# Fillers in the layer norms, eight-tile groups that end bank by bank, and the estimated mean taken off tile by tile

## The chip, the cores and the metric

The kernel runs on one core of a Trainium2 chip. The metric is the device time of one execution in microseconds (us). A core has engines that run side by side: TensorE (PE in the profile, PEld for its weight loads), VectorE (DVE), ScalarE (ACT), GpSimd (POOL) and SyncE (SP), whose queue issues the weight transfers here. Each engine works through its instructions in order and waits on semaphores for the others. PE's clock is granted by a throttle; the profile shows it as PEclk, as a share of full speed.

## The reference, cut to what matters

The kernel computes a decoder trunk of two layers on one sequence of 256 tokens with 2048 features, in float32. Each layer has a mixer and a feed-forward block, and after each of them the sum with the residual is normalised (post-norm):

```python
x = LN(alpha * x + gate * mixer(mod(x)))        # o0, o1: the mixer's output projection
x = LN(alpha * x + gate * swiglu(mod(x)))       # g.., d..: gate/up and down projections
mu  = mean(x); var = mean((x - mu) ** 2)
LN  = (x - mu) * rsqrt(var + 1e-5) * g + b
```

`mod` scales and shifts by vectors that come from the conditioning vector c (adaLN), and `gate` is one of them too. Layer 0's mixer is a forgetting attention beside a state-space layer, layer 1's a sliding-window attention with rotary positions. So there are four norms: after o0, after the feed-forward of layer 0 (ending with d01), after o1 and after d11. The first three feed a projection, the last one the output.

## The kernel before, in words

Everything is kept transposed: features lie in the 128 partitions, tokens in 256 columns, so the 2048 features are 16 tiles of 128 x 256 (`z`). The weights are streamed from HBM once, in pieces of 128 x 1024 float32 (512 KB) on SP's queue into a ring of nine buffers. Each piece is split into a rounded part `wh` (ACT, L269) and the rest `wl` (DVE, L270), and the activations lie in two parts `hi` and `lo` as well (`hp`). A product of a weight tile with an activation tile is then three passes of 256 columns: `wh*hi`, `wh*lo`, `wl*hi` (`mm3`, L609 to L611), or, where the output has a bank to itself, one pass of 512 columns and one of 256 (`mm2`, L614 and L615). In c1 and c2 the activations are the stationary side (L1346). A piece makes a **unit** of eight weight tiles; splits run two units ahead (`LOOK`), with three split buffers.

`_plan` lists the phases and their groups of output tiles: ..., o0, g00, d00, g01, d01, c1, c2, o1, g10, d10, g11, d11. Four PSUM banks of 512 columns accumulate (`acc`), and four (`aux`) serve everything else. Inside a group the tiles go k-outer (one k, all outputs, then the next k) or o-outer (one output to its end, then the next). An output tile is evacuated one unit after its last product (`c.later(1, ...)`): for o0, o1 and d.. tile by tile (`evac_slot`, then `z_evac`, which adds bank x gate to `z`, L950), for g.. as a whole group (`evac_group`, Silu on ACT and the product on DVE, L1279).

A **norm** runs while its sub-layer's outputs come in. After the first four tiles their mean is estimated (`ln_shift`: a product with ones, L986, a copy to SBUF, L988) and subtracted from all sixteen tiles in one burst of 16 subtractions (L992), since a shift by any constant leaves the norm as it is and keeps the sums of squares small. Then each tile is squared (ACT, L970) and added to the sums S1 and S2 (DVE, L976 to L980; `ln_stat`). After the last tile `ln_tail` brings the sums over the partitions with products of one column (L1008, `total`), forms the mean (L1031), the variance (L1033, L1034) and 1/sigma (ACT L1035; DVE L1037 to L1039), and spreads mean and 1/sigma over the partitions (L1013, `spread`). `ln_tile` then normalises tile by tile (L1055, L1064, L1067, L1068, L1075) into the next projection's `hp`. While it does so, nothing else is there for PE: the next projection waits for the first `hp`.

The order of instructions on each engine is set by a scheduler, which simulates a timeline and picks among what is ready; `c.front` gives an instruction a token (pe, act, front, load) by which those of one token keep their written order and go ahead of others. In the norm before c1, DVE also prepares the rotary positions (`rope_prep`, L1088 and on), whose input is loaded there by a transfer from ACT's queue (L1083).

## Time and profile before

| | |
|---|---|
| Time, three runs | 2271.1 us median (2271.01 to 2273.81) |
| The profiled execution | 2271.06 us; its span 2269.3 us, so 1.8 us lie around the span |
| Mean granted clock of PE | 0.988 |
| Busy: PE, DVE, ACT | 2214.3, 1705.1 and 1137.0 us (98%, 75%, 50%) |
| HBM read | 576.43 MB, 255 GB/s over the span |

A row of a group or of the timeline reads: start, duration, engine, line, operation, output <- inputs by the program's names, shape, the count of instructions joined in the row, and in brackets how long the engine stood idle before it and what released it. A row of a window reads: from:to, length, then for PE, PEld, DVE, ACT and POOL the busy time and the count, then PEclk, the share of the DMA engines that were busy and GB/s. Durations of PE overlap: products that take 0.28 us each start 0.12 us apart, so paces are read from start to start.

### The profile page before, as it was taken

Reading aid. Unit: us, or ns where it says so; the run is one execution under the profiler, and the core shown is the slowest. Engines: PE = TensorE matmul, PEld = TensorE weight load, DVE = VectorE, ACT = ScalarE, POOL = GpSimd, SP = SyncE. Lnnn points to the kernel's source line nnn. Section 1 sums busy time; section 2 is a strip of 40 time slices with the busy share of each in tenths; the row PEclk is TensorE's granted clock in tenths of the full one; section 3 lists DMA queues with packets and bytes.
Section 4 is the critical chain, followed back from the end, with each engine's and each line's share of the span. In section 5 each row is a group of like instructions: output and inputs, shape, how many; then the busy total and the mean of one; then the engine's idle time right before and its main releaser. Section 6 shows DMA issues by size and latency. Waiting matters only on the chain.

```text
span 2269.3 us, 37524 instructions
## 1 busy us (share of the span) xinstructions
PE 2214.3 (98%) x14362; PEld 1912.8 (84%) x14362; DVE 1705.1 (75%) x3026; ACT 1137.0 (50%) x1838; POOL 2.3 (0%) x6
## 2 busy tenths in 40 slices
PE   6999999999999999999999999999999999999997
PEld 4878887789888888888888878799888888888886
DVE  7649877888888888888886988787776555555576
ACT  3456565366444434444444766575444334444444
POOL 0000000000000000000000000000000000000000
PEclk8999999999999999999999999999999999999998
DMA  9988787858998889998874776358877556656662
GB/s 335 365 334 320 277 303 269 325 170 296 316 321 318 320 317 318 319 320 320 315 252 161 272 273 207 120 159 269 269 266 245 186 186 186 190 190 185 188 186 73
DMA packets 161476, 580.99 MB, mean 256 GB/s; under 512 B 18448, under 2 KB 18960, under 8 KB 160912
## 3 DMA queue, kind: packets, MB, share of 16 engines
q1 hardware_dynamic: 159984, 575.49, 73.7%
q10 hardware_dynamic: 1312, 3.11, 0.4%
q8 instruction: 112, 1.84, 0.3%
q14 instruction: 68, 0.56, 0.1%
HBM read 576.43 MB, written 2.10 MB: 255 GB/s over the span
## 4 chain that ended last, share of the span: by engine, by line
PE 93%; DVE 3%; ACT 2%; DMA 1%; issue 1%; ACTq 0%; SPq 0%; DVEq 0%
PE acc L614 43%; PE acc L615 22%; PE acc L1346 6%; PE acc L609 5%; PE acc L610 4%; PE acc L611 4%; PE ab L656 1%; PE aux L562 1%; DVE wl L270 1%; DVE w L540 1%; PE aux L1202 1%; PE aux L1169 0%; ACT wh L269 0%; DMA w<-in_ada 0%; PE tr L512 0%
## 5 line engine op out<-in xcount | busy, mean ns | idle before, releaser
L614 PE MATMUL acc<-hp,wh 128*128 128x512 f32 x4212 | 1465.3, 397 | 3.6 <-DVE z L950 2.4
L270 DVE TENSOR_TENSOR wl<-w,wh 128x1024 fp32r<-128x1024 f32 (+1 forms) x712 | 862.5, 1212 | 411.7 <-ACT wh L269 395.8
L269 ACT CAST wh<-w 128x1024 fp32r<-128x1024 f32 (+1 forms) x712 | 740.4, 1041 | 830.8 <-PE acc L614 462.5
L615 PE MATMUL acc<-hp,wl 128*128 128x256 f32 x4212 | 1149.3, 280 | 0.5 <-DVE wl L270 0.5
L614 PEld LDWEIGHTS acc<-hp,wh 128*128 128x128 f32 x4212 | 778.6, 188 | 180.9 <-ACT lnb L970 2.7
L615 PEld LDWEIGHTS acc<-hp,wl 128*128 128x128 f32 x4212 | 794.4, 189 | 19.9 <-DVE wl L270 1.6
L540 DVE CUSTOM_DVE_ANT_0 w<-w,crow 128x1024 f32<-128x1024 f32 x280 | 340.8, 1218 | 0.0
L610 PE MATMUL acc<-hp,wh 128*128 128x256 f32 x908 | 255.4, 288 | 0.0
L609 PE MATMUL acc<-hp,wh 128*128 128x256 f32 x908 | 249.2, 292 | 5.4 <-ACT hp L1068 2.3
L611 PE MATMUL acc<-hp,wl 128*128 128x256 f32 x908 | 245.5, 287 | 0.0
L609 PEld LDWEIGHTS acc<-hp,wh 128*128 128x128 f32 x908 | 170.8, 195 | 18.0 <-issue 6.7
L610 PEld LDWEIGHTS acc<-hp,wh 128*128 128x128 f32 x908 | 176.1, 194 | 5.1 <-issue 3.7
L611 PEld LDWEIGHTS acc<-hp,wl 128*128 128x128 f32 x908 | 170.5, 194 | 4.9 <-issue 3.8
L1346 PE MATMUL acc<-wh,hp 128*128 128x512 f32 x448 | 133.4, 398 | 1.1 <-ACT hp L1068 1.1
L950 DVE SCALAR_TENSOR_TENSOR z<-acc,mod,z 128x256 f32<-128x256 f32 x176 | 83.7, 481 | 39.9 <-PE acc L615 30.0
L1346 PEld LDWEIGHTS acc<-wh,hp 128*128 128x128 f32 x448 | 84.3, 190 | 21.2 <-issue 2.7
L1270 ACT COPY ftmp<-acc 128x256 f32<-128x256 f32 x80 | 29.8, 373 | 117.0 <-PE acc L615 117.0
L1346 PE MATMUL acc<-wl,hp 128*128 128x512 f32 x224 | 79.2, 399 | 0.4 <-DVE wl L270 0.4
L656 PE MATMUL ab<-w,cs 128*32 128x256 f32 x512 | 39.4, 416 | 18.4 <-ACT cs L321 11.3
L1271 DVE TENSOR_TENSOR ftmp<-acc,ftmp 128x256 f32<-128x256 f32 x80 | 33.8, 423 | 28.1 <-ACT ftmp L1270 28.1
L1346 PEld LDWEIGHTS acc<-wl,hp 128*128 128x128 f32 x224 | 42.3, 190 | 11.6 <-DVE wl L270 1.8
L656 PEld LDWEIGHTS ab<-w,cs 128*32 128x32 f32 x512 | 14.8, 115 | 29.5 <-ACT cs L321 11.3
(304 smaller groups left out, 1425.9 us busy)
## 6 DMA issues: line engine op xcount, KB each, us to landing
w<-in_w_gu SPq DMA_DIRECT2D x352, 512.0 KB, 4.3
w<-in_ada SPq DMA_DIRECT2D x320, 512.0 KB, 4.8
w<-in_w_dn SPq DMA_DIRECT2D x176, 512.0 KB, 3.8
w<-in_ada_s SPq DMA_DIRECT2D x64, 512.0 KB, 6.1
w<-in_w_ab SPq DMA_DIRECT2D x40, 512.0 KB, 5.3
w<-in_w_c SPq DMA_DIRECT2D x40, 512.0 KB, 4.2
w<-in_w_oab SPq DMA_DIRECT2D x32, 512.0 KB, 5.8
w<-in_w_oc SPq DMA_DIRECT2D x32, 512.0 KB, 4.3
```

Source lines behind the costliest of these rows:

```text
L269: self.front(nc.scalar.copy(wh[:, :n], src), "act")
L270: self.front(nc.vector.tensor_sub(wl[:, :n], src, wh[:, :n].bitcast(F32)))
L540: c.front(V.tensor_tensor_reduce(t, t, crow[:, 1024 * half:1024 * half + 1024], scale=1.0, scalar=0.0, op0=ALU.mult, op1=ALU.add, accum_ou ...
L609: PE.matmul(dst, lhsT=wh, rhs=hi_of(P, k), start=first, stop=False, skip_group_check=True)
L610: PE.matmul(dst, lhsT=wh, rhs=lo_of(P, k), start=False, stop=False, skip_group_check=True)
L611: PE.matmul(dst, lhsT=wl, rhs=hi_of(P, k), start=False, stop=last, skip_group_check=True)
L614: PE.matmul(bank, lhsT=wh, rhs=both_of(P, k), start=first, stop=False, skip_group_check=True)
L615: PE.matmul(bank[:, 256:512], lhsT=wl, rhs=hi_of(P, k), start=False, stop=last, skip_group_check=True)
L656: PE.matmul(abank[32 * j:32 * j + 32, 0:256], lhsT=cs[:, kk:kk + 32], rhs=t[:, 256 * j:256 * j + 256], start=(q == 0), stop=(q == 3), skip ...
L950: ins = V.scalar_tensor_tensor(zt(L, t), src, L["g"][:, t:t + 1], zt(L, t), op0=ALU.mult, op1=ALU.add)
L1271: V.tensor_tensor(gs, bg_[:, 0:256], gs, ALU.add)
L1346: PE.matmul(dst, lhsT=act[:, X], rhs=ww[:, c0:c0 + w], start=first, stop=(last and act is lo), skip_group_check=True)
```

## The change

It has three parts.

- **Fillers.** `ln_tail` takes a third aux bank and issues products of the identity with itself (128 x 128, float32) into it, which nothing reads: one between the last two totals, four behind the spread of the mean, six behind the spread of 1/sigma (`WARM`). This is done in the three norms that feed a projection. Totals, spreads and fillers get the token pe.
- **Groups of eight tiles.** In o1's first group and in the first group of g00 and of g10, the last two k go o-outer (`_k_outer_end`), so the four banks are finished one after another and not all in the last unit. A gate and an up tile are evacuated as soon as both are complete (`evac_group(g, only)`), no longer the whole group at once.
- **The estimated mean.** The job subtracts it from tiles 4 to 7 alone. Behind the addition of tile t, for t from 4 to 7, follow the subtraction and the sums of tile t - 4, and for t from 4 to 11 the subtraction of tile t + 4. Each of these subtractions is bound behind that addition by a dependency (`also_follow`). The sums now start with tile 4 and not with tile 0.

Nothing else is added: the number of subtractions, sums, splits and transfers is the same. The core of the diff (left out are two lines that only restate a condition):

```diff
+WARM = (1, 4, 6)
...
+def _k_outer_end(kts, ots):
+
+    return _k_outer(kts[:-2], ots) + _o_outer(kts[-2:], ots)
...
-            ph.append(("o1", [("oc", _k_outer(ks, list(range(8)))), ("oc", _o_outer(ks, [8, 9, 10, 11])),
+            ph.append(("o1", [("oc", _k_outer_end(ks, list(range(8)))), ("oc", _o_outer(ks, [8, 9, 10, 11])),
...
-                gs.append((gu, _k_outer(ks, [x for f in range(f0, f0 + n) for x in (f, 44 + f)])))
+                gs.append((gu, (_k_outer if n == 1 else _k_outer_end)(ks, [x for f in range(f0, f0 + n) for x in (f, 44 + f)])))
...
+    def also_follow(self, ins, other):
+
+        if other is not None:
+            self.tc.add_manual_dep(ins.ins, other.ins.name,
+                                   mybir.DependencyInfo(mybir.DependencyClass.Sync, mybir.DependencyReason.DATA),
+                                   reason="order")
...
                 ln_stat(L, t)
+                if t < 8:
+                    ln_shift_one(L, t - 4, ins)
+                    ln_stat(L, t - 4)
+                if t + 4 < KT:
+                    ln_shift_one(L, t + 4, ins)
...
-            if t == 0:
-                V.tensor_copy(L["S1"], zt(L, 0))
+            if t == 4:
+                V.tensor_copy(L["S1"], zt(L, t))
...
-            for t in list(range(4, KT)) + list(range(4)):
-                V.tensor_tensor(zt(L, t), zt(L, t), L["s"], ALU.subtract)
-                if t % 4 == 3:
-                    yield
-            for t in range(4):
-                ln_stat(L, t)
-                if t % 2:
-                    yield
+            for t in range(4, 8):
+                ln_shift_one(L, t)
+            yield
+
+        def ln_shift_one(L, t, behind=None):
+
+            c.also_follow(V.tensor_tensor(zt(L, t), zt(L, t), L["s"], ALU.subtract), behind)
...
+            i3, b3 = c.aux_get()
...
+            def warm(n):
+
+                for _ in range(n if nxt is not None else 0):
+                    c.front(PE.matmul(b3[:, 0:128], lhsT=ident, rhs=ident, start=True, stop=True, skip_group_check=True), "pe")
...
             total(b1, zt(L, KT - 1), False)
+            warm(WARM[0])
             total(b2, L["ring"][(KT - 1) % 2], False)
...
             L["wide"] = [spread(b1, m)]
+            warm(WARM[1])
...
             L["wide"].append(spread(b2, r))
+            warm(WARM[2])
+            c.aux_put(i3)
...
-        def evac_group(g):
+        def evac_group(g, only=None):
...
                 for i, o in enumerate(sorted(x for x in g.slot if x < 44)):
+                    if only not in (None, o):
+                        continue
...
+                    elif g.phase[0] == "g" and g.phase != "glu" and g.left[o % 44] == 0 and g.left[o % 44 + 44] == 0:
+                        c.later(1, lambda o=o: evac_group(g, o % 44))
```

How this moves instructions is seen best in the order of each engine. First PE in the norm before g00, before the change and after it (the numbers in names count buffers; `cst` holds the identity, `lna` the sums and small vectors, `lnb` the squares):

```order
L1008 MATMUL aux_5252<-ones_92,lna_4192 128x1 x2
L1008 MATMUL aux_5253<-ones_92,lna_4192 128x1 x2
L1008 MATMUL aux_5252<-ones_92,z_4189 128x1 x2
L1008 MATMUL aux_5253<-ones_92,lnb_4193 128x1 x2
L1013 MATMUL aux_5252<-cst_80,lna_4192 128x128 x2
L1013 MATMUL aux_5253<-cst_80,lna_4192 128x128 x2
L609 MATMUL acc_5315<-hp_5279,wh_5183 128x256
```

```order
L1026 MATMUL aux_5252<-ones_92,lna_4192 128x1 x2
L1026 MATMUL aux_5253<-ones_92,lna_4192 128x1 x2
L1026 MATMUL aux_5252<-ones_92,z_4189 128x1 x2
L1038 MATMUL aux_5254<-cst_80 128x128
L1026 MATMUL aux_5253<-ones_92,lnb_4193 128x1 x2
L1031 MATMUL aux_5252<-cst_80,lna_4192 128x128 x2
L1038 MATMUL aux_5254<-cst_80 128x128 x4
L1031 MATMUL aux_5253<-cst_80,lna_4192 128x128 x2
L1038 MATMUL aux_5254<-cst_80 128x128 x6
L622 MATMUL acc_5327<-hp_5291,wh_5183 128x256
```

The eleven fillers (L1038) stand among the totals (L1026) and the spreads (L1031), and ahead of the first product of g00 (L622). The norms before c1 and g10 have the same places.

Second, DVE in o1, around the subtraction of the estimated mean (`z` in two halves of eight tiles, `acc` the banks), before and after:

```order
L270 TENSOR_TENSOR wl_14821<-w_14515,wh_14820 128x1024
L992 TENSOR_TENSOR z_4188<-z_4188,lna_14025 128x256 x4
L992 TENSOR_TENSOR z_4189<-z_4189,lna_14025 128x256 x8
L992 TENSOR_TENSOR z_4188<-z_4188,lna_14025 128x256 x4
L950 SCALAR_TENSOR_TENSOR z_4188<-acc_14051,mod_16_106,z_4188 128x256
L950 SCALAR_TENSOR_TENSOR z_4188<-acc_14058,mod_16_106,z_4188 128x256 x2
L950 SCALAR_TENSOR_TENSOR z_4189<-acc_14781,mod_16_106,z_4189 128x256
L270 TENSOR_TENSOR wl_14849<-w_14545,wh_14848 128x1024
```

```order
L283 TENSOR_TENSOR wl_14819<-w_14509,wh_14818 128x1024
L1015 TENSOR_TENSOR z_4188<-z_4188,lna_14049 128x256 x5
L1015 TENSOR_TENSOR z_4189<-z_4189,lna_14049 128x256
L994 COPY lna_14049<-z_4188 128x256
L963 SCALAR_TENSOR_TENSOR z_4188<-acc_14075,mod_16_106,z_4188 128x256
L963 SCALAR_TENSOR_TENSOR z_4188<-acc_14082,mod_16_106,z_4188 128x256
L283 TENSOR_TENSOR wl_14841<-w_14539,wh_14840 128x1024
L963 SCALAR_TENSOR_TENSOR z_4188<-acc_14082,mod_16_106,z_4188 128x256
L995 COPY lna_14049<-lnb_14050 128x256
L963 SCALAR_TENSOR_TENSOR z_4189<-acc_14801,mod_16_106,z_4189 128x256
L997 TENSOR_TENSOR lna_14049<-lna_14049,z_4188 128x256
```

Six subtractions (L1015) and one copy now stand ahead of the next addition (L963), where sixteen stood before (L992, L950); behind the rows shown follow four subtractions, a split, two more subtractions and so on. On PE the product with ones moves 14 rows forward there.

Third, DVE at the end of the eight-tile group of g00 (`ftmp` holds the Silu, L540 and L553 are sums for a later adaLN vector), before and after:

```order
L1279 TENSOR_TENSOR ftmp_5302<-ftmp_5302,acc_5315 128x256
L1279 TENSOR_TENSOR ftmp_5302<-ftmp_5302,acc_5322 128x256
L544 TENSOR_TENSOR mod_15_105<-adap_5595,vec_75 128x4
L270 TENSOR_TENSOR wl_5894<-w_5717,wh_5893 128x1024
L1282 TENSOR_TENSOR hp_5303<-ftmp_5302,hp_5303 128x256 x2
```

```order
L1308 TENSOR_TENSOR ftmp_5314<-ftmp_5314,acc_5327 128x256
L283 TENSOR_TENSOR wl_5873<-w_5687,wh_5872 128x1024
L553 ISA w_5693,adap_5607<-w_5693,crow_100 128x1024
L553 ISA adap_5607 128x1
L1308 TENSOR_TENSOR ftmp_5314<-ftmp_5314,acc_5334 128x256
L1311 TENSOR_TENSOR hp_5315<-ftmp_5314,hp_5315 128x256
```

The two products that free the first two banks stood side by side; now the first (L1308) stands a split and a sum ahead of the second.

## The prediction

> **What bounds the kernel now.** I read the shares of the page and the chain of waits first, then the list of what TensorE (PE) waited for, then the windows with the granted clock, and only then the rows of the places that the change touches.

> ```profile
> PE 2214.3 (98%) x14362; PEld 1912.8 (84%) x14362; DVE 1705.1 (75%) x3026; ACT 1137.0 (50%) x1838; POOL 2.3 (0%) x6
> ...
> PE 93%; DVE 3%; ACT 2%; DMA 1%; issue 1%; ACTq 0%; SPq 0%; DVEq 0%
> ```

> PE is busy for 98% of the span and carries 93% of the chain that ends last. So a change can win in two ways only: it removes one of PE's few waits, or it makes PE's own work quicker. The waits that the change can reach are these (waiter, releaser: sum in us, times, longest):

> ```profile
> PE aux L1013 <- DVE lna L1039: 4.2, 4, 1.2
> PE acc L614 <- DVE z L950: 2.4, 1, 2.4
> PE acc L609 <- ACT hp L1068: 2.3, 2, 1.1
> PE aux L1013 <- DVE lna L1031: 1.5, 1, 1.5
> PE acc L614 <- DVE ftmp L1279: 1.2, 2, 0.9
> ```

> They are short: 4.2 us for the spread of 1/sigma in four norms, 2.4 for one bank in o1, 2.3 for the first normalised tile. But each has a second price, which busy time hides. These are windows at the edges on which the granted clock changes (duration; PE, PEld, DVE, ACT, POOL busy; then PEclk, DMA share, GB/s): first the norm before g00, then the one before c1, then the bank in o1, then the norm before g10.

> ```profile
> 485.44:488.85 3.41, 3.41 (x32) 3.41 (x31) 1.92 (x4) 0.44 (x2) 0.00 (x0) 1.00 0.55 175
> 488.85:492.27 3.42, 1.44 (x10) 1.05 (x9) 1.92 (x8) 0.81 (x3) 0.00 (x0) 1.00 0.25 103
> 492.27:495.68 3.41, 3.27 (x15) 3.27 (x16) 3.19 (x10) 3.10 (x8) 0.00 (x0) 0.50 0.02 5
> ...
> 1236.38:1239.79 3.41, 2.97 (x27) 2.88 (x26) 1.17 (x2) 0.42 (x1) 0.00 (x0) 1.00 0.58 203
> 1239.79:1243.20 3.41, 1.41 (x5) 1.11 (x6) 2.27 (x16) 0.29 (x1) 0.00 (x0) 0.50 0.09 35
> 1243.20:1246.62 3.42, 2.27 (x7) 1.78 (x8) 1.99 (x6) 1.63 (x4) 0.00 (x0) 0.50 0.00 0
> 1246.62:1250.03 3.41, 3.41 (x9) 2.64 (x9) 3.41 (x12) 3.35 (x8) 0.00 (x0) 0.50 0.00 0
> ...
> 1461.65:1465.07 3.42, 1.44 (x9) 0.97 (x7) 3.42 (x11) 1.77 (x3) 0.00 (x0) 1.00 0.17 67
> 1465.07:1468.48 3.41, 2.95 (x9) 2.59 (x10) 3.41 (x7) 0.00 (x0) 0.00 (x0) 0.50 0.00 0
> ...
> 1506.03:1509.44 3.41, 3.27 (x15) 3.27 (x16) 2.83 (x9) 2.74 (x8) 0.00 (x0) 0.50 0.01 2
> ```

> A window of 3.41 us in which PE is busy for 1.44 us is followed by one at half clock (488.85, 1461.65). At half clock, 2.27 us busy doesn't bring it back (1243.20), a full window does (1246.62, 3.27 at 492.27). The window from 1236.38 shows 2.97 busy and the clock still falls: in it stand the totals of the norm, products of one column, which count as busy on the page and, it seems, hardly for the clock.

> That is a mechanism of this trace. [...]

> **Fillers in the norms before g00 and g10.** PE's rows of the first:

> ```profile
> 487.17 0.95 PE L1008 MATMUL aux<-ones,lna 128*128 128x1 f32 x8
> 487.98 0.58 PE L1008 MATMUL aux<-ones,z 128*128 128x1 f32 x4
> 488.43 0.59 PE L1008 MATMUL aux<-ones,lnb 128*128 128x1 f32 x4
> 488.88 0.69 PE L1013 MATMUL aux<-cst,lna 128*128 128x128 f32 x4
> 490.55 0.71 PE L1013 MATMUL aux<-cst,lna 128*128 128x128 f32 x4 [0.98 <-DVE lna L1039]
> 492.41 1.22 PE L609 MATMUL acc<-hp,wh 128*128 128x256 f32 x4 [1.15 <-ACT hp L1068]
> ...
> 493.64 0.41 PE L611 MATMUL acc<-hp,wl 128*128 128x256 f32 x1
> 493.86 0.41 PE L609 MATMUL acc<-hp,wh 128*128 128x256 f32 x1
> ```

> Gain: products start every 0.21 us at half clock (493.64, 493.86) against 0.12 at full.

> ```profile
> 486.57 0.28 PE L610 MATMUL acc<-hp,wh 128*128 128x256 f32 x1
> 486.69 0.28 PE L611 MATMUL acc<-hp,wl 128*128 128x256 f32 x1
> ```

> From 492.41 to 495.68 that is 3.27 us, of which 0.09/0.21 = 43%, or 1.4 us, goes away at full clock. The norm before g10 has the same edges (3.27 busy in its cold window), so again 1.4.

> Price: a filler has the shape of the spread, 128 columns of f32. A spread is two calls (four records). It takes 0.69 us here and 1.22 at half clock (rows of c1, below). If the whole 0.53 of growth is the pass through the array, a call is 0.27 us at full clock; if a quarter of it is the pipeline's drain, 0.20. I take 0.24, an estimate, and 0.5 at half clock. The four fillers (0.96) fit in the gap of 0.98. The six (1.44) stand against 1.15, plus some 0.14 by which rows overlap (488.43 + 0.59 against 488.88): 0.15 late. The one between the two totals has no cover, since all that follows waits for the second total: 0.24. Net 1.4 - 0.4 = 1.0 per norm, **2.0 for both**; ends: -0.8 (fillers paid, clock falls all the same) to +2.8 (fillers hidden).

> **The norm before c1** differs: it starts late.

> ```profile
> 1240.12 0.17 DVE L1088 CAST kvrot<-kvrot 128x2 f32<-128x2 int32 x1 [1.93 <-DMA kvrot<-in_pos]
> ```

> ```profile
> 1240.82 1.22 PE L1013 MATMUL aux<-cst,lna 128*128 128x128 f32 x4 [1.47 <-DVE lna L1031]
> 1243.01 1.23 PE L1013 MATMUL aux<-cst,lna 128*128 128x128 f32 x4 [0.97 <-DVE lna L1039]
> 1245.38 1.22 PE L1346 MATMUL acc<-wh,hp 128*128 128x512 f32 x2 [1.15 <-ACT hp L1068]
> ```

> The cast of the positions waits 1.93 us for its transfer and stands ahead of the mean (L1031) on DVE; the change leaves that order. So there is a stretch of 1.47 us, with the totals before it, in which one filler stands. Whether the clock falls depends on how the window edges lie over it, which nothing fixes. If it holds, the products from 1245.38 to 1250.03 are no longer at half, which is 43% of 4.65 = 2.0 us, and the way from 1240.82 to the first product (4.56) shrinks to g00's 3.53 (488.88 to 492.41): 2.0 + 1.0 - 0.15 = 2.9. If it falls, the fillers run at 0.5 each: four take 2.0 against 0.97, six 3.0 against 1.15, which puts the first product up to 2.9 late, but the busy fillers bring the clock back sooner. By 1250.03 the kernel before has done 57% of 4.65 = 2.65 us of products (at full clock). With the clock back at 1246.62 the two spreads and ten fillers last to 1247.4, which leaves 2.6: nothing won. With the clock back at 1243.20 they last to 1245.7, which leaves 4.3: 1.6 won. Falls or holds, half and half: (0.8 + 2.9)/2, so **1.9**; ends -1.7 (half clock to 1250.03 all the same, and 57% of the 2.9 is lost) and 2.9.

> [...]

> **The estimated mean taken off tile by tile.** DVE and PE in o1:

> ```profile
> 1459.54 5.46 DVE L992 TENSOR_TENSOR z<-z,lna 128x256 f32<-128x256 f32 x16 [0.31 <-ACT lna L988]
> 1464.91 1.65 DVE L950 SCALAR_TENSOR_TENSOR z<-acc,mod,z 128x256 f32<-128x256 f32 x4
> ...
> 1465.53 0.76 PE L614 MATMUL acc<-hp,wh 128*128 128x512 f32 x1 [2.45 <-DVE z L950]
> ```

> Sixteen subtractions in one burst (0.34 us each) stand ahead of the additions that free a bank, and PE waits 2.45 us; then the clock is at half to 1468.48, 2.95 us, of which 43% is lost: 1.3. In the new order six subtractions and a copy (2.3 us) stand there: the addition starts near 1459.5 + 2.3 = 1461.8 even if the burst starts no sooner, and PE asks for the bank at 1463.1 (1465.53 - 2.45). So **3.7**, ends 0 (next bank late instead) and 3.8. The rest of the subtractions now stands behind additions, ahead of weight splits (`wl`, L270). From the order's rows, the two splits after the burst are done after 4.5 and 8.6 us of DVE work (subtractions, sums and copies at 0.34, and by the page's means

> ```profile
> L270 DVE TENSOR_TENSOR wl<-w,wh 128x1024 fp32r<-128x1024 f32 (+1 forms) x712 | 862.5, 1212 | 411.7 <-ACT wh L269 395.8
> ...
> L950 DVE SCALAR_TENSOR_TENSOR z<-acc,mod,z 128x256 f32<-128x256 f32 x176 | 83.7, 481 | 39.9 <-PE acc L615 30.0
> ```

> 1.21 for a split and 0.48 for an addition): at 1464.0 and 1468.1. PE takes 8 tiles of three passes of 0.12, 2.9 us a unit, so they are wanted at 1463.1 + 2.9 = 1466.0 and at 1468.9: 0.8 us of margin at the tighter one.

> In o0, d01 and d11 the burst costs PE no wait on a bank, so nothing is won there. DVE has little room in two of them:

> ```profile
> 430.00:440.00 10.00, 9.25 (x55) 6.61 (x54) 10.00 (x17) 4.29 (x7) 0.00 (x0) 1.00 0.70 254
> ...
> 1160.00:1170.00 10.00, 9.83 (x57) 8.34 (x56) 10.00 (x21) 4.70 (x7) 0.00 (x0) 1.00 0.94 312
> ```

> The count of operations is the same, only spread over more units, so I put this at 0. Ends: +0.9 (PE's idle in these windows, 0.75 and 0.17, goes) and -13.6 (third rival).

> **Groups that end bank by bank.**

> ```profile
> 541.05 0.50 PE L614 MATMUL acc<-hp,wh 128*128 128x512 f32 x1 [0.88 <-DVE ftmp L1279]
> ...
> 1554.23 0.50 PE L614 MATMUL acc<-hp,wh 128*128 128x512 f32 x1 [0.29 <-DVE ftmp L1279]
> ```

> After the eight-tile group the first bank was finished in the last unit with all the others, and its evacuation made PE wait 0.88 and 0.29 us. Now that bank's products end three banks earlier: 30 products of 0.12 us = 3.6 us, and its evacuation is queued on its own. **1.2**, ends 0 and 1.2.

> **Sum.** 2.0 + 1.9 + 3.7 + 1.2 = 8.8 us. The profiled execution took 2271.06 us (span 2269.3 and 1.8 outside it), the median of the runs is 2271.1, so one stands for the other: 2271.1 - 8.8 = **2262.3 us**.

> **Rivals.** (1) **The fillers don't hold the clock.** For it: products of one column seem not to count, so a window's share isn't the page's busy time, and the norm still has 1.7 us of totals and, in c1, a late transfer. Against it: ten fillers nearly close the window of 1.44 us. Then the two g norms pay 0.4 each and c1 1.7, and only o1 and the group ends win: -4.9 + 0.8 + 1.7 = -2.4, **2268.7**. (2) **The wait in o1 only moves**, to the next bank or to a split behind four subtractions in a row; for it: DVE is without a pause from 1459.54 on; against it: the 0.8 us of margin above. 8.8 - 3.7 = 5.1: **2266.0**. (3) **Slower: additions dragged behind DVE's queue.** Behind the additions of tiles 4 to 11 now stand 12 subtractions (4.1 us at 0.34) and the sums of four more tiles (2.7 us, eight at 0.34), 6.8 us a norm. Where DVE is 10 of 10 busy, splits and later additions come that much late. It decides once the lateness passes the two units that splits run ahead (5.6 us). Worst: 13.6 in o0 and d01, and o1 wins nothing: 13.6 - 5.1 = +8.5, **2279.6**. Against it: the burst put 5.46 us at one place, and PE lost at most 0.75 us by it there.

> **How the numbers follow.** Forecast 0.62 (its own range 2259 to 2265, by c1's and o1's ends), rival 1 0.16, rival 2 0.10, rival 3 0.06, mixtures between the forecast and rival 1 0.06. All upper ends together are 11.6 us (2259.5); the range goes 1 us beyond, for what no row shows, and up to 2269.0, just above rival 1. It leaves out rival 3, a part of rival 1 and the tails. A difference under 0.2%, 4.5 us, can't be told from none. Faster by more: forecast, rival 2 (5.1), the mixtures and a small part of rival 1, 0.79; within: the rest of rival 1, 0.15; slower 0.06.

> **What would show it.** The windows after the norms before g00 and g10 at clock 1.00 and the first products 0.12 apart; in c1 either that or half clock ending one window sooner; no wait of PE on L950's successor in o1 above 0.3 us; no wait on the gate products at the ends of the eight-tile groups. The forecast is wrong if PE waits for splits in o0 or d01, or if the clock at the norms is at half with the fillers running.

## The result, and the profile after

| | before | changed |
|---|---|---|
| Time | 2272.1 us median of 4 (2271.01 to 2273.81) | 2257.24 us median of 4 (2256.14 to 2258.75) |
| Profiled execution | 2271.06 us, span 2269.3 | 2256.14 us, span 2254.3 |
| Mean granted clock of PE | 0.988 | 0.993 |

The ratio is 0.9933, 95% interval 0.9917 to 0.9949: 15 us less. The forecast was 2262.3 us, range 2258.5 to 2269.0. The sign was right; the time lies just below the range, and the gain is 1.7 times the forecast.

What PE waited for, in the changed kernel (us in total, times, longest):

```profile
PE aux L1214 <- ACT pb L1217: 2.1, 2, 1.3
PE aux L1031 <- DVE lna L1064: 1.2, 1, 1.2
...
PE acc L1377 <- DVE wl L283: 0.6, 2, 0.4
...
PE aux L575 <- DMA w<-in_ada: 0.3, 1, 0.3
PE aux L1031 <- DVE lna L1055: 0.3, 1, 0.3
```

The wait on a bank in o1 (2.4 before), both waits on gate products (1.2), the waits for the first normalised tile (3.4) and three of the four waits on 1/sigma are gone from this list; the 1.2 left is the last norm, which has no fillers. The attention's wait (2.1) is as before.

PE in the norm before g00, and the windows around the norms before g00, c1 and g10:

```profile
487.07 0.58 PE L1026 MATMUL aux<-ones,z 128*128 128x1 f32 x4
487.52 0.47 PE L1038 MATMUL aux<-cst 128*128 128x128 f32 x2
487.83 0.50 PE L1026 MATMUL aux<-ones,lnb 128*128 128x1 f32 x4
488.19 0.69 PE L1031 MATMUL aux<-cst,lna 128*128 128x128 f32 x4
488.72 1.06 PE L1038 MATMUL aux<-cst 128*128 128x128 f32 x8
489.86 0.71 PE L1031 MATMUL aux<-cst,lna 128*128 128x128 f32 x4
490.40 1.50 PE L1038 MATMUL aux<-cst 128*128 128x128 f32 x12
491.72 0.74 PE L622 MATMUL acc<-hp,wh 128*128 128x256 f32 x4
492.30 0.28 PE L623 MATMUL acc<-hp,wh 128*128 128x256 f32 x1
492.42 0.28 PE L624 MATMUL acc<-hp,wl 128*128 128x256 f32 x1
```

```profile
486.70:490.11 3.41, 3.33 (x29) 3.14 (x29) 1.54 (x8) 0.71 (x2) 0.00 (x0) 1.00 0.47 154
490.11:493.53 3.42, 3.42 (x31) 3.42 (x31) 2.56 (x7) 2.15 (x6) 0.00 (x0) 1.00 0.02 5
...
1234.22:1237.64 3.42, 3.05 (x25) 2.77 (x25) 2.26 (x16) 0.50 (x2) 0.00 (x0) 1.00 0.40 147
1237.64:1241.05 3.41, 3.41 (x24) 3.10 (x23) 2.61 (x8) 2.19 (x6) 0.00 (x0) 1.00 0.00 0
...
1490.22:1493.64 3.42, 3.34 (x29) 3.15 (x28) 2.29 (x8) 1.31 (x4) 0.00 (x0) 1.00 0.02 6
```

The clock stays at 1.00 through all three norms, and the first products of g00 start 0.12 us apart. From the first spread (488.19) to the first product (491.72) it is 3.53 us, as before: the six fillers (1.32 us, 490.40 to 491.72) end just when the first tile is ready.

DVE in o1, where the burst of 5.46 us stood:

```profile
1448.19 2.11 DVE L1015 TENSOR_TENSOR z<-z,lna 128x256 f32<-128x256 f32 x6 [0.66 <-ACT lna L1006]
1450.20 0.29 DVE L994 COPY lna<-z 128x256 f32<-128x256 f32 x1
1450.41 0.88 DVE L963 SCALAR_TENSOR_TENSOR z<-acc,mod,z 128x256 f32<-128x256 f32 x2
```

PE goes on without a wait there, at full clock.

**Where the time went.** I set starts of the same instruction side by side, before and changed, and note the lead of the changed kernel; the growth of the lead from mark to mark is what a stage won. A *wide product* is a pass of 512 columns (`mm2`), a *g norm* the norm before g00 or before g10, a *cold window* a window of 3.41 us at half clock. All stages below are read from one profile of each kernel.

| mark | before | changed | lead | won since the mark above |
|---|---|---|---|---|
| o0, 63rd wide product | 437.54 | 437.49 | 0.1 | |
| first total before g00 | 487.17 | 486.26 | 0.9 | o0: 0.9 |
| g00, 61st product `wh*hi` | 515.17 | 513.44 | 1.7 | its norm: 0.8 |
| first wide product of g00 | 541.05 | 538.28 | 2.8 | the end of the group: 1.0 |
| d01, 95th wide product | 1155.61 | 1152.60 | 3.0 | 0.2 |
| first total before c1 | 1237.51 | 1233.29 | 4.2 | d01: 1.2 |
| c1, 37th product | 1255.82 | 1248.24 | 7.6 | its norm: 3.4 |
| first wide product of o1 | 1451.18 | 1442.31 | 8.9 | c2 and the attention: 1.3 |
| first total before g10 | 1500.93 | 1487.53 | 13.4 | o1: 4.5 |
| g10, 61st product `wh*hi` | 1528.93 | 1514.72 | 14.2 | its norm: 0.8 |
| first wide product of g10 | 1554.23 | 1539.56 | 14.7 | the end of the group: 0.5 |
| last product | 2254.47 | 2239.55 | 14.9 | 0.3 |

The forecast's own terms (two g norms, c1, o1, group ends) make 11.0 of it, against 8.8; 3.9 us lie in stages that it put at nothing.

### The profile page after: what moved, and what is told of

It reads as the page before. It is cut to its first block, busy times and chain, and to the rows that moved or that the text cites. A ratio compares the mean times of both kernels' runs of the same rounds, so it can differ in the third digit from the quotient of the medians.

```text
span 2254.3 us, 37633 instructions
## 1 busy us (share of the span) xinstructions
PE 2209.0 (98%) x14428; PEld 1912.5 (85%) x14428; DVE 1703.9 (76%) x3026; ACT 1137.4 (50%) x1838; POOL 2.3 (0%) x6
## 4 chain that ended last, share of the span: by engine, by line
PE 93%; DVE 4%; ACT 1%; issue 1%; DMA 1%; ACTq 0%; DVEq 0%
PE acc L627 44%; PE acc L628 22%; PE acc L1377 5%; PE acc L622 4%; PE acc L624 4%; PE acc L623 4%; PE ab L669 1%; PE aux L575 1%; DVE wl L283 1%; DVE w L553 1%; PE aux L1229 1%; PE aux L746 1%; PE aux L1196 0%; PE aux L1214 0%; PE tr L525 0%
## 5 line engine op out<-in xcount | busy, mean ns | idle before, releaser
L553 DVE CUSTOM_DVE_ANT_0 w<-w,crow 128x1024 f32<-128x1024 f32 x280 | 341.2, 1220 | 0.0
L623 PE MATMUL acc<-hp,wh 128*128 128x256 f32 x908 | 252.4, 286 | 0.0
L622 PE MATMUL acc<-hp,wh 128*128 128x256 f32 x908 | 245.4, 289 | 3.9 <-ACT hp L680 2.7
L622 PEld LDWEIGHTS acc<-hp,wh 128*128 128x128 f32 x908 | 167.8, 192 | 15.8 <-issue 5.9
L963 DVE SCALAR_TENSOR_TENSOR z<-acc,mod,z 128x256 f32<-128x256 f32 x176 | 84.2, 482 | 38.8 <-PE acc L628 30.6
L669 PEld LDWEIGHTS ab<-w,cs 128*32 128x32 f32 x512 | 14.7, 115 | 30.9 <-ACT cs L334 11.5
```

What stands on the lines that cost most here:

```text
L553: c.front(V.tensor_tensor_reduce(t, t, crow[:, 1024 * half:1024 * half + 1024], scale=1.0, scalar=0.0, op0=ALU.mult, op1=ALU.add, accum_ou ...
L622: PE.matmul(dst, lhsT=wh, rhs=hi_of(P, k), start=first, stop=False, skip_group_check=True)
L623: PE.matmul(dst, lhsT=wh, rhs=lo_of(P, k), start=False, stop=False, skip_group_check=True)
L669: PE.matmul(abank[32 * j:32 * j + 32, 0:256], lhsT=cs[:, kk:kk + 32], rhs=t[:, 256 * j:256 * j + 256], start=(q == 0), stop=(q == 3), skip ...
L963: ins = V.scalar_tensor_tensor(zt(L, t), src, L["g"][:, t:t + 1], zt(L, t), op0=ALU.mult, op1=ALU.add)
```

## The experiments

Twelve kernels ran. All the times of the kernel before, beside these and beside the changed kernel, lie between 2268.65 and 2277.56 (37 runs, median 2272.6). Profiles differ already ahead of the first norm, which no part of the change touches: the first mark (437.54 before) stood 3.8 us later in the profile of the kernel without fillers, 3.9 in that with fillers in the g norms alone and 3.6 in that with half the fillers. These are the three in which the clock is at half for 10.24 us from 54 or 55 us on; in the kernel before it is for 3.41 there, in the changed one not at all. Their lag is at most 0.5 us at 49 us and whole at 66. So I read the stages by the marks of the table, from which that falls out, and the medians only for the whole.

### Each part alone

The fillers alone:

```diff
 (before)
+WARM = (1, 4, 6)
...
+            warm(WARM[0])
...
+            warm(WARM[1])
...
+            warm(WARM[2])
```

Totals and spreads have their token here as well.

> The kernel before with the fillers alone (one, four and six in each of the three norms); the estimated mean is still taken off in a burst and the eight-tile groups end as before. Theory (the fillers keep the clock at full through the norms): the windows after the norms before g00, c1 and g10 show clock 1.00, each g norm wins 0.8 us and c1's 2 to 3.4, the wait on a bank in o1 stays at about 2.4 us with its half clock: 3.6 to 5 us less than before, 2266 to 2268.5. Rival (the clock held in the changed kernel only because the window edges lay well, and the fillers only cost): the clock falls in at least one g norm, and the time is within 1.5 us of before.

Measured: 2264.76 us median of 4 (2262.0 to 2266.46), ratio 0.9961 (0.9945 to 0.9976). The clock is at 1.00 through all three norms; they win 0.8, 3.1 and 0.8 us. o1 still waits, and its clock still falls. The chain of effects is the theory's; the median lies 1.2 us under its lower end. The token by itself doesn't keep the clock: in the kernels below that keep it and have no fillers of 128 columns in a norm, the clock falls to 0.50 there.

The mean tile by tile alone:

```diff
 (before)
+                if t < 8:
+                    ln_shift_one(L, t - 4, ins)
+                    ln_stat(L, t - 4)
+                if t + 4 < KT:
+                    ln_shift_one(L, t + 4, ins)
...
-            for t in list(range(4, KT)) + list(range(4)):
-                V.tensor_tensor(zt(L, t), zt(L, t), L["s"], ALU.subtract)
...
+            for t in range(4, 8):
+                ln_shift_one(L, t)
```

> The kernel before with the mean taken off tile by tile alone, no fillers, groups as before. Theory (the burst was what made PE wait in o1, in o0 for the adaLN transfer at 439 us, and in d01 for two splits): no wait on a bank in o1, none of 0.7 us in o0 and of 0.5 us in d01; 4 us won in o1, 0.9 in o0 and 1.1 in d01, 6 us in all, 2265 to 2266.5; the clock still falls in the norms. Rival (o1's wait goes through the groups that end bank by bank, not through the mean): o1 still waits over 1 us and the gain is under 2.5 us.

Measured: 2265.51 us median of 6 (2263.99 to 2270.0), ratio 0.9971 (0.9958 to 0.9983). No wait on a bank in o1, which wins 3.8 us; d01 wins 1.2, o0 0.9. The rival falls. Two things weren't expected. The g norms lost 1.0 us each against the kernel before: there the clock stayed at half for two windows, not one. And the attention won 3.6 us, though no line of it is changed (below).

The groups that end bank by bank alone:

```diff
 (before)
-            ph.append(("o1", [("oc", _k_outer(ks, list(range(8)))), ("oc", _o_outer(ks, [8, 9, 10, 11])),
+            ph.append(("o1", [("oc", _k_outer_end(ks, list(range(8)))), ("oc", _o_outer(ks, [8, 9, 10, 11])),
...
-                gs.append((gu, _k_outer(ks, [x for f in range(f0, f0 + n) for x in (f, 44 + f)])))
+                gs.append((gu, (_k_outer if n == 1 else _k_outer_end)(ks, [x for f in range(f0, f0 + n) for x in (f, 44 + f)])))
...
+                        c.later(1, lambda o=o: evac_group(g, o % 44))
```

> The kernel before with the eight-tile groups ending bank by bank alone. Theory (only the two waits on the gate products go): 1.0 us at the end of g00's group and 0.4 at g10's, o1's wait on a bank stays within 0.5 us: 1 to 2 us less, about 2270. Rival (in o1 the banks finished earlier take the wait away as well, burst or not): o1 waits under 1 us, 4 us more are won, about 2266.

Measured: 2264.99 us median of 7 (2262.48 to 2270.02), ratio 0.9966 (0.9955 to 0.9977). The group ends win 1.0 and 0.5, as expected. But o1 won 2.9 us as well, half way to the rival: the wait on a bank is gone with the burst still there,

```profile
1452.08 5.46 DVE L997 TENSOR_TENSOR z<-z,lna 128x256 f32<-128x256 f32 x16 [0.66 <-ACT lna L993]
1457.45 1.27 DVE L955 SCALAR_TENSOR_TENSOR z<-acc,mod,z 128x256 f32<-128x256 f32 x3
...
1458.63 1.22 DVE L275 TENSOR_TENSOR wl<-w,wh 128x1024 fp32r<-128x1024 f32 x1
```

and the waits are now on the splits that stand behind it (PE in o1):

```profile
PE acc L619 <- ACT wh L274: 0.5, 1, 0.5
PE acc L620 <- DVE wl L275: 0.4, 1, 0.4
```

So two of the three parts take away one and the same wait. The attention won 3.6 us here too; the g norms lost 1.0 and 1.5 us, again with two cold windows.

### All but one part

Without the fillers:

```diff
-WARM = (1, 4, 6)
...
-            warm(WARM[0])
...
-            warm(WARM[1])
...
-            warm(WARM[2])
```

The third bank and the token of totals and spreads go with them.

> The changed kernel without its fillers (the mean tile by tile and the groups that end bank by bank remain). Theory (fillers keep the clock; without them what a norm costs hangs on where the window edges lie): half clock after the norms before g00, c1 and g10, against the changed kernel 0.8 to 2 us more in each g norm and 2 to 4 us in c1's, o1 without its wait on a bank; 4 to 7 us more than the changed kernel in all, 2261 to 2264.5, about 10 us under the kernel before. Rival (the parts add up as they did one by one: 8.3 + 5.9 us of the two profiles): 2257 us, no slower than the changed kernel.

Measured: 2264.74 us median of 9 (2263.4 to 2268.32), ratio 0.9967 (0.9957 to 0.9977). The norms lose 1.2, 0.5 and 0.8 us against the kernel before, where the changed kernel won 0.8, 3.4 and 0.8; o1 wins its 4.5. So in the changed kernel the fillers are worth 7.5 us by the medians, half of the whole, and in the profiles 7.5 in the norms and 1.3 in the attention. Of the 3.9 of this that lie before c1, 1.3 aren't the fillers': the positions landed 3.5 us after their issue in this profile and 2.2 in the changed kernel's, and DVE needs them ahead of the mean. The mean and the group ends together (7.6 us) are worth no more than either alone (7.5, 8.0): the rival falls.

Without the groups that end bank by bank, and with the burst as before:

```diff
 (changed; the first of the two)
-            ph.append(("o1", [("oc", _k_outer_end(ks, list(range(8)))), ("oc", _o_outer(ks, [8, 9, 10, 11])),
+            ph.append(("o1", [("oc", _k_outer(ks, list(range(8)))), ("oc", _o_outer(ks, [8, 9, 10, 11])),
...
-                gs.append((gu, (_k_outer if n == 1 else _k_outer_end)(ks, [x for f in range(f0, f0 + n) for x in (f, 44 + f)])))
+                gs.append((gu, _k_outer(ks, [x for f in range(f0, f0 + n) for x in (f, 44 + f)])))
```

The second puts `ln_shift` and the sums back as they were before.

> The changed kernel without the groups that end bank by bank (fillers and the mean tile by tile remain). Theory (for what it still adds, that part is worth the two waits on the gate products alone, since the mean taken off tile by tile frees o1's bank by itself): PE waits about 0.9 and 0.3 us on the gate products after the groups of g00 and g10, no wait on a bank in o1, 1.0 to 1.5 us more than the changed kernel, 2258 to 2259.5. Rival (the gain in o1 needs both): o1 waits again over 0.5 us, 3 us or more lost, over 2260.

> The changed kernel with the mean taken off in a burst as before (fillers and groups that end bank by bank remain). Theory (the earlier banks take about 2.4 of the 3.9 us in o1 by themselves, the tile-by-tile mean the rest, and it also takes away PE's waits on splits in d01): o1 wins about 1.5 us less than in the changed kernel, d01 1.1 less: 2 to 4 us more than the changed kernel, 2259 to 2261. Rival (the three parts simply add, as their single gains of about 8 us each would have it): 7 to 8 us more, 2264 to 2265.

Measured: 2262.95 us (2262.65 to 2263.78) and 2263.64 us (2259.79 to 2264.38), medians of 4. Without the group ends the gate products wait again (1.2 us in two places), as the theory had it, and o1's bank waits for nothing; but o1 wins 0.7 us less, and the totals before g10 wait 0.9 us for the last sums:

```profile
PE aux L1021 <- DVE lna L993: 0.6, 1, 0.6
PE aux L1021 <- DVE lna L992: 0.3, 1, 0.3
```

In this norm the clock fell in spite of its fillers, and it lost 1.4 us in place of 0.8 won. The time is 3.5 us over the theory's upper end: the rival's place is wrong and its size about right. With the burst, o1 won 2.8 and d01 0.1 (the theory had 1.5 and 1.1 less: 1.7 and 1.1 measured), and the clock fell before c1 in spite of the fillers, where 1.8 were won and not 3.4; so the time is 2.6 us over the theory's upper end. In d11 the three of these kernels that have the burst lose 1.0 us against the kernel before. No wait is listed there; over the last 165 output tiles the wide products start every 353.3 ns in place of 346.7 (the kernel with the fillers alone). Why the pace differs isn't shown. The simple addition of three gains of 8 us falls.

### The binding

```diff
-            c.also_follow(V.tensor_tensor(zt(L, t), zt(L, t), L["s"], ALU.subtract), behind)
+            V.tensor_tensor(zt(L, t), zt(L, t), L["s"], ALU.subtract)
```

> The changed kernel without the binding of the subtractions behind the additions (the scheduler may place each subtraction anywhere after the estimate is there). Theory (the binding is what keeps the additions that free a bank ahead of the subtractions): the scheduler puts subtractions in a row ahead of additions again, o1 waits 1 to 2.4 us for a bank and loses 1.5 to 4 us: 2259 to 2261. Rival (it is enough that the subtractions are written tile by tile): within 1 us of the changed kernel, 2256 to 2258.5.

Measured: 2262.37 us median of 4 (2258.93 to 2264.87), ratio 0.995 (0.9933 to 0.9967). The scheduler puts eleven subtractions ahead of the first addition in o1 (six with the binding), and o1 wins 2.7 in place of 4.5. The loss there, 1.8 us, is in the range expected; the median lies 1.4 us over its upper end. The place is a little other: PE waits in o1 not for the bank but for a split (first row), the second rival of the prediction. The second row stands in d01: without the binding the subtractions gather there too, and PE waits for `wl` twice, as in the kernel before:

```profile
PE acc L627 <- ACT wh L282: 0.8, 1, 0.8
PE acc L628 <- DVE wl L283: 0.5, 2, 0.3
```

### What keeps the clock

Without the first filler, with half of the fillers, and with fillers of one column:

```diff
-WARM = (1, 4, 6)
+WARM = (0, 4, 6)    # the first kernel; (0, 2, 3) the second
```

```diff
-                for _ in range(n if nxt is not None else 0):
-                    c.front(PE.matmul(b3[:, 0:128], lhsT=ident, rhs=ident, start=True, stop=True, skip_group_check=True), "pe")
+                for _ in range(2 * n if nxt is not None else 0):
+                    c.front(PE.matmul(b3[:, 0:1], lhsT=ident, rhs=ident[:, 0:1], start=True, stop=True, skip_group_check=True), "pe")
```

> The changed kernel without the one filler between the last two totals (four and six remain). Theory (that filler has no cover and costs 0.21 us in each g norm, and the share of the window is made by the others): clock 1.00 through all three norms, 0.2 us sooner from totals to first product in the norms before g00 and g10, 0.4 us less in all, not to be told from the changed kernel by its time. Rival (the filler breaks up the stretch of one-column products and the clock needs it): half clock after one of the norms, 1 to 3 us more.

> The changed kernel with two fillers behind the spread of the mean and three behind that of 1/sigma, none between the totals. [...] Rival (the gaps must be filled whole): half clock after at least two norms.

> The changed kernel with fillers of one column in place of 128, twice as many of them, so that they take about the same time and show as busy on the page. Theory (one-column products hardly count for the clock): the windows of the norms show PE busy for 3 us or more of 3.41 and the clock still falls after all three norms, as in the kernel before. Rival (what counts is that PE has an instruction at work): clock 1.00 through the norms, the time of the changed kernel, 2256 to 2259.

Without the first filler: 2256.74 us median of 4 (2255.84 to 2260.66), the clock at full, the g norms 1.0 won in place of 0.8: the price of that filler was 0.2 us each, and it isn't needed. With half of them (one time, 2260.48 us) the clock holds before g00 and g10, each norm wins 1.0, and it falls before c1, where the positions come late: the window from 1235.42, with 3.18 us of 3.42 busy, is followed by two at 0.50. That is half clock after one norm, not after two: the rival falls. With fillers of one column it falls after all three norms (one time, 2277.35 us; it is slower also because the fillers themselves came out longer, 2.36 us for the 16 records behind the spread of the mean against 1.06 for the changed kernel's 8):

```profile
489.14 2.36 PE L1038 MATMUL aux<-cst 128*128 128x1 f32 x16
491.36 1.20 PE L1031 MATMUL aux<-cst,lna 128*128 128x128 f32 x4
492.35 5.12 PE L1038 MATMUL aux<-cst 128*128 128x1 f32 x24
497.33 1.20 PE L622 MATMUL acc<-hp,wh 128*128 128x256 f32 x4
```

```profile
486.87:490.28 3.41, 3.41 (x32) 3.41 (x33) 1.56 (x8) 0.71 (x2) 0.00 (x0) 1.00 0.42 156
490.28:493.69 3.41, 3.41 (x18) 3.41 (x18) 0.84 (x3) 0.64 (x2) 0.00 (x0) 0.50 0.02 5
493.69:497.11 3.42, 3.42 (x17) 3.42 (x18) 3.31 (x10) 3.10 (x8) 0.00 (x0) 0.50 0.00 0
497.11:500.50 3.39, 3.39 (x17) 3.39 (x18) 3.39 (x9) 3.39 (x7) 0.00 (x0) 0.50 0.00 0
```

A window in which PE is busy for all of its 3.41 us by the profile (486.87) is followed by one at half clock, and two windows at half clock, as full (490.28, 493.69), are followed by half clock again; in the kernel before one full window of products of 512 columns did bring it back (1246.62, PE 3.41 of 3.41, then 1.00 from 1250.03 on). So here it isn't enough that PE has an instruction at work. The products that start in the window from 486.87 take 1076 columns, those in the changed kernel's window from 486.70, which full clock follows, 4118 (how they are counted stands in the last section). The theory on fillers of one column holds, its rival falls.

### The norm before c1

Fillers in the g norms alone, and, the other way, the positions loaded early:

```diff
-                for _ in range(n if nxt is not None else 0):
+                for _ in range(n if nxt is not None and not (l == 0 and kind == 1) else 0):
```

```diff
 (with WARM = (0, 4, 6))
-            posi = m[:, 1856:1858].bitcast(I32)
-            nc.scalar.dma_start(posi, I["pos"])
+            posi = S["posi"]
...
         def hook_glu():
...
+            S["posi"] = c.small(2, "posi", I32)
+            nc.scalar.dma_start(S["posi"], I["pos"])
```

> The changed kernel with fillers in the norms before g00 and g10 alone, none before c1. Theory (c1's norm is where the fillers win most, 3 to 4 us, since the late positions leave a long idle stretch there; the order of the attention behind it moves with them and is worth another 1 us): half clock after the norm before c1 and 4 to 5 us more than the changed kernel, 2261 to 2262.5. Rival (the three norms are worth the same, about 1 to 2 us each): 1 to 2 us more, 2258 to 2259.5.

> The changed kernel without the filler between the totals, and with the positions loaded into a buffer of their own during the earlier layer, so that the cast ahead of the mean waits for no transfer in the norm before c1. Theory (that wait is all that sets c1's norm apart from the others): from totals to first product 5.0 us before c1 as in the norms before g00 and g10 (5.2 with that filler), against 5.9 in the changed kernel; the clock at full through all norms; about 1.3 us less than the changed kernel, 2255.5 to 2256.5. Rival (DVE's work on the rotary angles is what holds the mean up): 5.6 us or more, and the time of the changed kernel.

Fillers in the g norms alone: 2260.97 us median of 4 (2259.58 to 2263.69), 3.7 us more than the changed kernel. The clock falls before c1 for two windows, and the norm loses 0.2 against the kernel before where the changed kernel wins 3.4. That is near the theory's size, but 2.0 of the 3.5 go with the positions, which landed 4.2 us after their issue in this profile; 1.5 are left for the fillers. The theory's second half is wrong: the attention won 1.3 us all the same.

Positions early: 2256.85 us median of 5 (2253.92 to 2259.51), ratio 0.9929 (0.9917 to 0.9942), not to be told from the changed kernel's 0.9933. From the first total to the first product it is 5.23 us (1233.35 to 1238.58, from the marks), as in the g norms without that filler (5.24), against 5.90 in the changed kernel, and the norm wins 4.0. The step is as expected (the 5.0 expected was a slip: 5.24 is also the kernel before's time in the norm before g00); half a microsecond is under what the runs can show.

### The attention, which nobody changed

No edit touches c2 or the attention, and yet the stage from c1's 37th product to o1's first wide one (o1's first eight tiles are in it too) won: 1.3 us in the changed kernel, 1.1 with the fillers alone, 3.6 with the mean or the group ends alone, nothing without the fillers, 1.3 with fillers in the g norms alone, 2.7 with early positions. Two things make this up. The scheduler sets another order: on PE 541 calls stand between the last product of c2 and the first wide one of o1 before and in both kernels without fillers before c1 that hold the other two parts, 544 in the changed kernel and all that have fillers of 128 columns there, 531 with the mean or the group ends alone, where PE's waits in this stretch fall from

```profile
PE aux L1187 <- ACT pb L1190: 2.1, 2, 1.3
```

to

```profile
PE aux L1198 <- DVE pb L890: 0.8, 2, 0.5
PE aux L1213 <- ACT pb L1201: 0.3, 1, 0.3
```

The other is the clock. The idle stretch at the end of the attention falls into one window in the kernel before and in the changed one, and over two in the kernel with early positions, in which PE, DVE and ACT have the same order here as in the changed kernel (before; changed; early positions):

```profile
1430.93:1434.35 3.42, 1.22 (x7) 0.65 (x6) 2.96 (x15) 3.42 (x13) 0.00 (x0) 1.00 0.50 153
1434.35:1437.76 3.41, 3.31 (x18) 2.41 (x20) 0.94 (x1) 2.27 (x7) 0.00 (x0) 0.50 0.40 109
```

```profile
1421.95:1425.37 3.42, 1.43 (x9) 0.69 (x7) 2.96 (x16) 3.42 (x13) 0.00 (x0) 1.00 0.39 153
1425.37:1428.78 3.41, 3.09 (x16) 2.33 (x18) 1.15 (x1) 2.26 (x7) 0.00 (x0) 0.50 0.31 84
```

```profile
1419.93:1423.34 3.41, 2.32 (x18) 1.81 (x17) 3.26 (x14) 3.41 (x17) 0.00 (x0) 1.00 0.25 34
1423.34:1426.75 3.41, 2.18 (x19) 1.57 (x21) 2.30 (x7) 3.41 (x9) 0.00 (x0) 1.00 0.30 121
```

With early positions the clock holds, with PE busy for 2.32 and 2.18 us of the two windows against 1.43 us of the one in the changed kernel, and 1.4 us more are won (2.7 against 1.3). As the order is the same, I put these down to where the window's edges fall. Two kernels with 541 calls and one order differ by as much (nothing won with a cold window, 1.3 without). The other profiles fit: seven kernels with 544 calls and a cold window won 1.0 to 1.4, the two with 531 and none 3.6. So the 1.3 us of the changed kernel, whose window is cold as before, come from the order.

## Why the prediction was right or wrong, point by point

- **"Fillers in the norms before g00 and g10": 2.0 for both, measured 1.6.** The mechanism was right: the clock holds at 1.00. The price of a filler, taken at 0.24 us, was 0.22 (1.32 for six), so six were not late; the filler without cover cost its 0.2. The clock gave the 1.4 in full: the lead is 0.7 at the first product of g00 and 2.1 at the 16th. Then 0.4 are lost at the 57th: PE, which now gets there sooner, waits for a split that DVE, between the norm's tiles, ends at 498.78:

```profile
497.56 1.22 DVE L283 TENSOR_TENSOR wl<-w,wh 128x1024 fp32r<-128x1024 f32 x1
```

```profile
498.42 0.28 PE L623 MATMUL acc<-hp,wh 128*128 128x256 f32 x1
498.83 0.39 PE L624 MATMUL acc<-hp,wl 128*128 128x256 f32 x1
```

 The same 0.4 is lost at the same product in both g norms of the kernels with fillers alone, without the first filler and with early positions. The sum has no term for it.
- **"The norm before c1": 1.9, measured 3.4.** It took "falls or holds" half and half; the clock held, which was priced at 2.9 and gave 3.1 (1.0 from the first spread to the first product, 2.1 in the first eleven products). Two things were not in the price. The positions landed 2.2 us after their issue, not 3.1 (DVE waited 0.98 us, not 1.93), which is the 0.95 that the lead grows from first total to first spread; and 0.7 are lost again to late splits, 0.5 of it here:

```profile
1246.31 0.73 PE L1377 MATMUL acc<-wl,hp 128*128 128x512 f32 x2 [0.20 <-DVE wl L283]
```

 The 0.95 is luck as far as the forecast goes: issued there, the transfer takes 2.0 to 4.2 us in the profiles. In the kernel with fillers, group ends and the burst (2.9 us for the transfer) the clock did fall here (2.45 us of PE in the window from 1236.58, then 0.50), for one window in place of three, and the norm won 1.8; the prediction had 1.6 for that case.
- **"The estimated mean", o1: 3.7, measured 4.5.** The wait and its half clock are 3.9 to 4.1 of it; the rest came in small steps over the stage. The span of 0 to 3.8 that it was given was too narrow. Not seen at all was that the group ends take most of the same wait.
- **"In o0, d01 and d11 the burst costs PE no wait on a bank, so nothing is won there ... I put this at 0": the step that failed first.** d01 won 1.2 us in each of the nine kernels whose mean comes off tile by tile and bound, and 0.1 in each of the three others that keep the burst: that is shown. The burst made splits late, and PE waited for `wl`, 0.33 and 0.17 us in the trace:

```profile
1158.31 0.39 PE L615 MATMUL acc<-hp,wl 128*128 128x256 f32 x1 [0.33 <-DVE wl L270]
...
1161.32 0.39 PE L615 MATMUL acc<-hp,wl 128*128 128x256 f32 x1 [0.17 <-DVE wl L270]
```

 From start to start these gaps are 0.5 and 0.3 us over the usual pace, more than the 0.17 of idle time that I read from the busy time of a window: PE's rows overlap, so a window's busy time hides a part of each wait. In all nine the lead grows by 0.6 and 0.4 us at these two places, 1.0 of the 1.2. Without the binding both waits are back (0.33 and 0.16 us) and the lead doesn't grow there; the 1.1 us which that kernel still won in d01 come later and evenly, by a quicker pace whose cause isn't shown. The upper end of +0.9 for this term counted 0.75 for o0 and 0.17 for d01; the two stages won 0.9 and 1.2.

 In o0 0.9 were won. PE's wait for the adaLN transfer is 0.7 us before and isn't in the list of that stage after; but kernels with the burst won 0.3 to 0.8 there too, so how much is the mean's stays open.
- **"Groups that end bank by bank": 1.2, measured 1.5.** Right, with the rest from the first of the two places (1.0 for 0.88).
- **No term at all for the attention.** The change moves the order there, and 1.3 us were won; it needed a bound of its own, some 3.5 us wide, since two builds with one part each moved it by 3.6.
- **The range.** It summed the upper ends of the named terms (11.6) and went 1 us beyond. With d01's 1.2 and the attention's, it would have reached 2256.
- **The rivals.** Fillers that don't hold the clock: no in the changed kernel, but it fell in spite of fillers in three others (two late sums before g10 in one; half the fillers, or a later transfer of the positions, before c1). These stood beside it; they weren't tested one by one. A wait in o1 that moves to a split: not in the changed kernel, but seen without the binding and with the group ends alone. DVE too full behind the additions: no stage shows it.

## What to carry to other kernels

Where a kernel is bound by PE, list the windows after which the clock falls, not only the waits: here a stretch with two gaps of about 1 us (0.98 and 1.15) and some one-column products cost another 1.4 us at half clock, and ten products of 128 columns into a spare bank saved it. Then look at what PE meets sooner: here a split on DVE took 0.4 us back. A burst of cheap operations on an engine that also feeds PE is best tied to the operations that free a buffer, and bound there, or a scheduler will gather it again. And if parts of a change each win 8 us alone, that says little of their sum: here two removed the same wait, and each moved an order that neither touched.
